# Sums of tail tokens on GpSimd, chunk-wide first products and a reshuffled tail in a weighted expert sum

## The chip, the cores and the metric

The kernel runs on one core of a Trainium2 chip. The metric is device time in microseconds (us) of one execution, the median of ten runs. A profile of one execution shows what each engine does: TensorE (PE; its weight loads are shown as PEld), VectorE (DVE), ScalarE (ACT), GpSimd (POOL) and SyncE (SP, which only issues transfers here). A name with a "q" behind it (DVEq, SPq, ACTq) is the engine's instruction queue. Transfers between the device memory (HBM) and the core's memory (SBUF) are moved by 16 DMA engines. TensorE writes its results to a memory of its own, PSUM.

## The reference

For each of 16 x 1024 = 16384 tokens there are the outputs of 8 experts, 512 numbers each, and 8 weights. The result is the weighted sum over the experts, in float32:

```python
batch, seq, n_experts, expert_dim = 16, 1024, 8, 512
weights = combine_weights[..., np.newaxis]
return np.sum(expert_outputs * weights, axis=2).astype(np.float32)
```

The input has 268.4 MB, the output 33.6 MB.

## The kernel before

Each of the 128 partitions handles 128 tokens. The first 120 of them (LOOP) are worked on in 12 rounds of R = 10, the last 8 (TAIL) in a tail. All instructions of all engines are written out by hand, with semaphores between the engines; each engine works through its list in order.

The tile ring holds the inputs of ten tokens per partition (10 x 8 x 512 numbers) and is the only input buffer. A round is loaded in three chunks of 4, 4 and 2 tokens (CHUNKS). SyncE issues a chunk's load (line 109) as soon as VectorE has finished the same chunk of the round before (semaphore done, raised once per finished token), so loads run ahead by as much as VectorE has already released. The tile acc holds 20 tokens' results, two halves for two rounds. ScalarE copies a round's weights to w_c (line 145) and issues the store of a finished half (line 99); before a half of acc is written again, its store must have landed (semaphore stored). In before VectorE itself waits for that, as for the chunks, in the helper take (line 173).

VectorE works on pairs of tokens. For the two tokens of a pair it alternates, expert by expert: the first product (line 204, one tensor operand and one weight per partition), then seven fused operations (line 187, called fused below: input times weight plus the sum so far). A fused operation waits for the semaphore step of the one two places earlier, which wrote the sum that it reads. Five pairs make a round: 80 instructions.

The tail's 8 tokens go to ring slots 0 to 7. SyncE issues their loads (line 119) one by one, each when the last round has released its slot. TensorE sums four of the eight terms of every tail token (line 163): the stationary operand is a diagonal matrix with one weight per token, made by ScalarE from an identity matrix (line 151; five buffers, made ahead as far as they are free), and the moving operand is the token's row; the sum is in ps, in PSUM. VectorE adds the other four by fused operations, the first of which reads ps. SyncE then issues the store of round 11 and four tail stores (line 123) of 4, 2, 1 and 1 tokens, in this order, on the same queue as the loads. GpSimd only builds the identity matrix at the start (lines 128 and 129).

Of the kernel before, what the change touches and what calls it, by code (L numbers as in the profile page):

```python
# [10 lines left out]
def kernel(  # L11
# [18 lines left out]
    nc = tc.nc  # L30
    fp32 = mybir.dt.float32
    mult, add = mybir.AluOpType.mult, mybir.AluOpType.add

    B, S, E, D = expert_outputs.shape
    T = B * S
    P = 128
    R = 10
# [4 lines left out]
    LOOP = GROUPS * G  # L42
    TAIL = T_P - LOOP
    ROUNDS = LOOP // R
# [11 lines left out]
    x_t = x[cut:T].rearrange("(p j) e d -> p j e d", j=TAIL)  # L56
# [1 line left out]
    o_t = o[cut:T].rearrange("(p j) d -> p j d", j=TAIL)  # L58


    pe_e = [4] * TAIL
    tail_loads = [(j, 1) for j in range(TAIL)]
    tail_stores = [(0, 4), (4, 2), (6, 1), (7, 1)]

    order = []
    for q in ((0, 1), (2,), (3,), (4,), (5,), (6,), (7,)):
        order += [(j, e) for e in range(pe_e[q[0]], E) for j in q]
    diags = [(j, e) for j in range(TAIL) for e in range(pe_e[j])]

    one = ctx.enter_context(tc.tile_pool(name="one", bufs=1))  # L70
# [1 line left out]
    ring = one.tile([P, R, E, D], fp32, name="ring")  # L72
    acc = one.tile([P, G, D], fp32, name="acc")
    w_t = one.tile([P, T_P, E], fp32, name="w_t")
    w_c = one.tile([P, G, E], fp32, name="w_c")
    ident = one.tile([P, P], fp32, name="ident")
    diag = one.tile([P, DIAGS, P], fp32, name="diag")
    ps = psum.tile([P, TAIL, D], fp32, name="ps")

    sem = tc.alloc_semaphore  # L80
    w_in = sem("w_in")
    w_set = [sem(f"w_set{h}") for h in range(2)]
    loaded = [sem(f"loaded{c}") for c in range(C)]
    stored = [sem(f"stored{h}") for h in range(2)]
    step = sem("step")
    done = sem("done")
    tail_in = [sem(f"tail_in{k}") for k in range(len(tail_loads))]
    tail_out = sem("tail_out")
    id_set = sem("id_set")
    diag_set = sem("diag_set")  # L90
    product = sem("product")

    def load_of(j):
        return [k for k, (q, m) in enumerate(tail_loads) if q <= j < q + m][0]

    def store(queue, n):
        h = n % 2
        queue.wait_ge(done, (n + 1) * R)
        queue.dma_start(
            out=o_g[n // 4, n // 2 % 2, :, h * R : h * R + R], in_=acc[:, h * R : h * R + R]  # L100
        ).then_inc(stored[h], 16)

    def loads_and_last_stores(sync):
        for n in range(ROUNDS):
            for c, (r, m) in enumerate(CHUNKS):
                if n:
                    sync.wait_ge(done, (n - 1) * R + r + m)
                g = n % 2 * R + r
                sync.dma_start(
                    out=ring[:, r : r + m], in_=x_g[n // 4, n // 2 % 2, :, g : g + m]  # L110
                ).then_inc(loaded[c], 16)
                if n == 0 and c == 0:
                    sync.dma_start(
                        out=w_t[:, 0:LOOP].rearrange("p (n m) e -> p n m e", m=M), in_=w_g
                    ).then_inc(w_in, 16)
                    sync.dma_start(out=w_t[:, LOOP:T_P], in_=w_x).then_inc(w_in, 16)
        for k, (j, m) in enumerate(tail_loads):
            sync.wait_ge(done, LOOP - R + j + m)
            sync.dma_start(out=ring[:, j : j + m], in_=x_t[:, j : j + m]).then_inc(tail_in[k], 16)
        store(sync, ROUNDS - 1)  # L120
        for j, m in tail_stores:
            sync.wait_ge(done, LOOP + j + m)
            sync.dma_start(out=o_t[:, j : j + m], in_=acc[:, j : j + m]).then_inc(tail_out, 16)
        sync.wait_ge(stored[(ROUNDS - 1) % 2], 16)
        sync.wait_ge(tail_out, 16 * len(tail_stores))

    def identity(gpsimd):
        gpsimd.memset(ident, 0.0).then_inc(id_set, 1)  # L128
        gpsimd.affine_select(  # L129
            out=ident,  # L130
            in_=ident,
            compare_op=mybir.AluOpType.not_equal,
            fill=1.0,
            base=0,
            pattern=[[-1, P]],
            channel_multiplier=1,
        ).wait_op(id_set, 1, "sem-ge").then_inc(id_set, 1)

    def weights_and_stores(scalar):
        scalar.wait_ge(w_in, 32)  # L140
        for n in range(ROUNDS):
            if n >= 2:
                store(scalar, n - 2)
            h = n % 2
            scalar.copy(  # L145
                out=w_c[:, h * R : h * R + R], in_=w_t[:, n * R : n * R + R]
            ).then_inc(w_set[h], 1)
        store(scalar, ROUNDS - 2)
        scalar.wait_ge(id_set, 2)
        for k, (j, e) in enumerate(diags):  # L150
            i = scalar.mul(out=diag[:, k % DIAGS], in_=ident, mul=w_t[:, LOOP + j, e : e + 1])  # L151
            i.then_inc(diag_set, 1)
            if k >= DIAGS:
                i.wait_op(product, k - DIAGS + 1, "sem-ge")

    def first_terms(tensor):
        came = set()
        for k, (j, e) in enumerate(diags):
            if load_of(j) not in came:
                came.add(load_of(j))  # L160
                tensor.wait_ge(tail_in[load_of(j)], 16)
            tensor.wait_ge(diag_set, k + 1)
            tensor.matmul(  # L163
                ps[:, j],
                lhsT=diag[:, k % DIAGS],
                rhs=ring[:, j, e],
                start=e == 0,
                stop=e == pe_e[j] - 1,
            ).then_inc(product, 1)

    def terms(vector):
        def take(s, v):
            vector.wait_ge(s, v).then_inc(s, -v)  # L173

        last = {}

        def count(i, g, e):

            if e == E - 1:
                i.then_inc(done, 1)  # L180
            else:
                i.then_inc(step, 1)
                last["all"] = last.get("all", 0) + 1
                last[g] = last["all"]

        def fused(g, e, weight, before):
            return vector.scalar_tensor_tensor(  # L187
                out=acc[:, g], in0=ring[:, g % R, e], scalar=weight, in1=before, op0=mult, op1=add
            )

        for h in range(2):
            vector.sem_inc(stored[h], 16)
        with nc.Fori(0, GROUPS, engines=OrderedEngineSet([vector.engine])):
            for h in range(2):
                take(w_set[h], 1)
                take(stored[h], 16)
                for c, (r, m) in enumerate(CHUNKS):
                    take(loaded[c], 16)
                    for q in range(h * R + r, h * R + r + m, 2):
                        for e in range(E):  # L200
                            for g in (q, q + 1):
                                weight = w_c[:, g, e : e + 1]
                                if e == 0:
                                    i = vector.tensor_scalar_mul(  # L204
                                        out=acc[:, g], in0=ring[:, g % R, 0], scalar1=weight
                                    )
                                else:
                                    i = fused(g, e, weight, acc[:, g])
                                    i.wait_op(step, last[g], "sem-ge")
                                count(i, g, e)  # L210
            take(step, last["all"])

        last.clear()
        came = set()
        take(stored[0], 16)
        vector.wait_ge(w_in, 32)
        for j, e in order:
            weight = w_t[:, LOOP + j, e : e + 1]
            if load_of(j) not in came:
                came.add(load_of(j))  # L220
                vector.wait_ge(tail_in[load_of(j)], 16)
            if e == pe_e[j]:
                i = fused(j, e, weight, ps[:, j])
                i.wait_op(product, sum(pe_e[: j + 1]), "sem-ge")
            else:
                i = fused(j, e, weight, acc[:, j])
                i.wait_op(step, last[j], "sem-ge")
            count(i, j, e)

    with tc.tile_critical(no_gpsimd_drain=True):  # L230
        loads_and_last_stores(nc.sync)
        identity(nc.gpsimd)
        weights_and_stores(nc.scalar)
        first_terms(nc.tensor)
        terms(nc.vector)
# [30 lines left out]
```

## Time and profile before

| what | value |
|---|---|
| median of 10 runs | 707.92 us (707.63 to 708.38) |
| the profiled execution's own time | 707.72 us |
| its span in the profile | 705.9 us |
| busy: VectorE | 628.2 us, 992 instructions |
| busy: TensorE | 31.4 us, 64 instructions |
| busy: ScalarE | 16.7 us, 45 instructions |
| busy: GpSimd | 0.7 us, 6 instructions |
| DMA | 302.5 MB, mean 429 GB/s |
| issues of the tail stores | from 684.7 to 700.4 us; 4.1 us (last) to 16.3 us (first) to landing |
| SyncE's final wait | ends at 704.4 us |

The span is the time between the first and the last event of the profiled execution; its own time has 1.8 us around it. In the page's groups a line reads: source line, engine, operation, output <- inputs, shapes, count | busy time in us, mean ns of one instruction | idle time of the engine just before, and what ended most of it. Consecutive VectorE instructions overlap in part, so that a group's time is less than count times mean; the spacing of the starts is the better price. The row of DMA shares divides the span in 40 slices, a digit is the busy share in tenths.

### The profile page before, as it was taken

To read this page: it belongs to the slowest core of one execution; us is meant where nothing else is said; L and a number is where in the kernel's file an instruction comes from. 1 tells how busy PE (TensorE), PEld (TensorE's weight loads), DVE (VectorE), ACT (ScalarE), POOL (GpSimd) and SP (SyncE) were. 2 spreads that over 40 slices of the span, in tenths; PEclk is the share of its full clock that TensorE was granted. 3 is DMA by queue.
4 is the path that set the end of the run, shared out by engine and by line. 5 is a ranking of instruction groups with operands and counts; after the bars stand their busy time and mean duration, and the time that the engine had idled before them with its cause. 6 is when DMAs were issued, how large, how long until landed. Compare 5 with 4: busy or idle time off the path is not lost. (4 is left out here: it accounts for less than half of the span.)

```text
span 705.9 us, 1388 instructions
## 1 busy us (share of the span) xinstructions
PE 31.4 (4%) x64; PEld 12.4 (2%) x64; DVE 628.2 (89%) x992; ACT 16.7 (2%) x45; POOL 0.7 (0%) x6
## 2 busy tenths in 40 slices
PE   0000000000000000000000000000000000000664
PEld 0000000000000000000000000000000000000221
DVE  0599989979979979979979989998997997997994
ACT  0000000000000000000000000000000000000230
POOL 0000000000000000000000000000000000000000
PEclk9999999999999999999999999999999999999998
DMA  9999999999999999999999999999999999999997
GB/s 416 386 472 420 406 424 447 416 444 436 432 433 449 438 405 438 436 424 473 434 395 452 417 427 438 468 395 467 420 445 416 431 430 461 427 432 404 430 428 331
DMA packets 9186, 302.53 MB, mean 429 GB/s; under 512 B 1120, under 2 KB 1504, under 8 KB 1888
## 3 DMA queue, kind: packets, MB, share of 16 engines
q1 hardware_dynamic: 7600, 273.68, 90.0%
q10 hardware_dynamic: 1584, 28.84, 9.5%
q14 instruction: 2, 0.02, 0.0%
HBM read 268.96 MB, written 33.55 MB: 429 GB/s over the span
## 5 line engine op out<-in xcount | busy, mean ns | idle before, releaser
L187 DVE SCALAR_TENSOR_TENSOR acc<-ring,w_c,acc 128x512 f32<-128x512 f32 x840 | 561.4, 744 | 0.0
L204 DVE TENSOR_SCALAR acc<-ring,w_c 128x512 f32<-128x512 f32 x120 | 52.6, 480 | 68.1 <-DVEq L173 68.1
L163 PE MATMUL ps<-ring,diag 128*128 128x512 f32 x64 | 31.4, 638 | 665.8 <-DMA ring<-in_expert_outputs_dram 665.8
L163 PEld LDWEIGHTS ps<-ring,diag 128*128 128x128 f32 x64 | 12.4, 202 | 684.0 <-DMA ring<-in_expert_outputs_dram 671.0
L187 DVE SCALAR_TENSOR_TENSOR acc<-ring,w_t,acc 128x512 f32<-128x512 f32 x24 | 17.6, 749 | 0.6
L145 ACT COPY w_c<-w_t 128x80 f32<-128x80 f32 x12 | 3.0, 258 | 559.9 <-DVE acc L187 537.8
L151 ACT ACTIVATE diag<-ident,w_t 128x128 f32<-128x128 f32 x32 | 12.4, 399 | 114.4 <-PE ps L163 60.2
L187 DVE SCALAR_TENSOR_TENSOR acc<-ring,w_t,ps 128x512 f32<-128x512 f32 x8 | 5.9, 742 | 3.4 <-PE ps L163 3.4
L145 ACT ACT_TABLE_LOAD x1 | 1.3, 1283 | 0.9 <-SPq L230 0.9
L129 POOL TENSOR_SCALAR_AFFINE_SELECT ident<-ident 128x128 f32<-128x128 f32 x1 | 0.3, 293 | 0.1
L128 POOL MEMSET ident<- 128x128 f32 x1 | 0.2, 206 | 0.5 <-SPq L230 0.5
L250 POOL MEMSET const-bfloat16-1.0<- 128x1 bf16 x1 | 0.1, 102 | 0.0
L250 POOL MEMSET const-uint8-127<- 128x1 uint8 x1 | 0.1, 102 | 0.0
L250 POOL MEMSET const-float32-0.0<- 128x1 f32 x1 | 0.1, 99 | 0.2 <-issue 0.2
L250 POOL MEMSET const-float32-1.0<- 128x1 f32 x1 | 0.1, 99 | 0.0
## 6 DMA issues: line engine op xcount, KB each, us to landing
ring<-in_expert_outputs_dram SPq DMA_DIRECT2D x12, 4096.0 KB, 34.4
out_dram<-acc ACTq DMA_DIRECT2D x11, 2560.0 KB, 26.5
ring<-in_expert_outputs_dram SPq DMA_DIRECT2D x8, 2048.0 KB, 30.1
out_dram<-acc SPq DMA_DIRECT2D x1, 2560.0 KB, 26.2
out_dram<-acc SPq DMA_DIRECT2D x1, 1024.0 KB, 16.3
out_dram<-acc SPq DMA_DIRECT2D x1, 512.0 KB, 11.1
out_dram<-acc SPq DMA_DIRECT2D x2, 256.0 KB, 5.5
w_t<-in_combine_weights_dram SPq DMA_DIRECT2D x1, 480.0 KB, 22.7
```

The costliest lines, as they stand in the source:

```text
L128: gpsimd.memset(ident, 0.0).then_inc(id_set, 1)
L129: gpsimd.affine_select(out=ident, in_=ident, compare_op=mybir.AluOpType.not_equal, fill=1.0, base=0, pattern=[[-1, P]], channel_multiplier ...
L145: scalar.copy(out=w_c[:, h * R : h * R + R], in_=w_t[:, n * R : n * R + R]).then_inc(w_set[h], 1)
L151: i = scalar.mul(out=diag[:, k % DIAGS], in_=ident, mul=w_t[:, LOOP + j, e : e + 1])
L163: tensor.matmul(ps[:, j], lhsT=diag[:, k % DIAGS], rhs=ring[:, j, e], start=e == 0, stop=e == pe_e[j] - 1,).then_inc(product, 1)
L187: return vector.scalar_tensor_tensor(out=acc[:, g], in0=ring[:, g % R, e], scalar=weight, in1=before, op0=mult, op1=add)
L204: i = vector.tensor_scalar_mul(out=acc[:, g], in0=ring[:, g % R, 0], scalar1=weight)
L250: nc = _bacc.Bacc("TRN2", target_bir_lowering=False, num_devices=1)
```

## The change

In the loop, the first products of a whole chunk become one multiply of two tensors, the second of them the weights repeated along the row (a broadcast). VectorE no longer waits for stores to land; ScalarE does, before it copies the weights into a half.

In the tail, GpSimd computes tokens 0 and 1 alone (new function pooled_tokens): eight products per token, written back into the ring, then a tree of 4, 2 and 1 adds; the semaphore pooled counts the finished tokens, and SyncE waits for both before the store of tokens 0 to 3. It begins when the even rounds' stores have all landed and the token is loaded. TensorE sums five terms of tokens 2 to 6 and four of token 7, VectorE the other three and four. For token 7 VectorE's own sum begins with a product and no longer waits for TensorE; TensorE's sum is added at the end.

```diff
--- before.py
+++ after.py
@@ -58,13 +58,9 @@
     o_t = o[cut:T].rearrange("(p j) d -> p j d", j=TAIL)
 
 
-    pe_e = [4] * TAIL
-    tail_loads = [(j, 1) for j in range(TAIL)]
+    POOLED = 2
+    pe_e = [0, 0, 5, 5, 5, 5, 5, 4]
     tail_stores = [(0, 4), (4, 2), (6, 1), (7, 1)]
-
-    order = []
-    for q in ((0, 1), (2,), (3,), (4,), (5,), (6,), (7,)):
-        order += [(j, e) for e in range(pe_e[q[0]], E) for j in q]
     diags = [(j, e) for j in range(TAIL) for e in range(pe_e[j])]
 
     one = ctx.enter_context(tc.tile_pool(name="one", bufs=1))
@@ -84,14 +80,13 @@
     stored = [sem(f"stored{h}") for h in range(2)]
     step = sem("step")
     done = sem("done")
-    tail_in = [sem(f"tail_in{k}") for k in range(len(tail_loads))]
+    tail_in = [sem(f"tail_in{j}") for j in range(TAIL)]
     tail_out = sem("tail_out")
     id_set = sem("id_set")
+    pool_step = sem("pool_step")
+    pooled = sem("pooled")
     diag_set = sem("diag_set")
     product = sem("product")
-
-    def load_of(j):
-        return [k for k, (q, m) in enumerate(tail_loads) if q <= j < q + m][0]
 
     def store(queue, n):
         h = n % 2
@@ -114,14 +109,16 @@
                         out=w_t[:, 0:LOOP].rearrange("p (n m) e -> p n m e", m=M), in_=w_g
                     ).then_inc(w_in, 16)
                     sync.dma_start(out=w_t[:, LOOP:T_P], in_=w_x).then_inc(w_in, 16)
-        for k, (j, m) in enumerate(tail_loads):
-            sync.wait_ge(done, LOOP - R + j + m)
-            sync.dma_start(out=ring[:, j : j + m], in_=x_t[:, j : j + m]).then_inc(tail_in[k], 16)
+        for j in range(TAIL):
+            sync.wait_ge(done, LOOP - R + j + 1)
+            sync.dma_start(out=ring[:, j], in_=x_t[:, j]).then_inc(tail_in[j], 16)
         store(sync, ROUNDS - 1)
         for j, m in tail_stores:
-            sync.wait_ge(done, LOOP + j + m)
+            if j < POOLED:
+                sync.wait_ge(pooled, POOLED)
+            sync.wait_ge(done, LOOP - POOLED + j + m)
             sync.dma_start(out=o_t[:, j : j + m], in_=acc[:, j : j + m]).then_inc(tail_out, 16)
-        sync.wait_ge(stored[(ROUNDS - 1) % 2], 16)
+        sync.wait_ge(stored[(ROUNDS - 1) % 2], 16 * ROUNDS // 2)
         sync.wait_ge(tail_out, 16 * len(tail_stores))
 
     def identity(gpsimd):
@@ -136,16 +133,42 @@
             channel_multiplier=1,
         ).wait_op(id_set, 1, "sem-ge").then_inc(id_set, 1)
 
+    def pooled_tokens(gpsimd):
+        gpsimd.wait_ge(w_in, 32)
+        gpsimd.wait_ge(stored[0], 16 * ROUNDS // 2)
+        steps = 0
+        for j in range(POOLED):
+            gpsimd.wait_ge(tail_in[j], 16)
+            for e in range(E):
+                gpsimd.tensor_scalar(
+                    out=ring[:, j, e],
+                    in0=ring[:, j, e],
+                    scalar1=w_t[:, LOOP + j, e : e + 1],
+                    scalar2=None,
+                    op0=mult,
+                ).then_inc(pool_step, 1)
+            for m in (4, 2, 1):
+                steps += {4: E, 2: 4, 1: 2}[m]
+                for k in range(m):
+                    y = acc[:, j] if m == 1 else ring[:, j, k]
+                    i = gpsimd.tensor_tensor(
+                        out=y, in0=ring[:, j, k], in1=ring[:, j, m + k], op=add
+                    )
+                    i.wait_op(pool_step, steps, "sem-ge")
+                    i.then_inc(pooled if m == 1 else pool_step, 1)
+
     def weights_and_stores(scalar):
         scalar.wait_ge(w_in, 32)
         for n in range(ROUNDS):
+            h = n % 2
             if n >= 2:
                 store(scalar, n - 2)
-            h = n % 2
+                scalar.wait_ge(stored[h], 16 * (n // 2))
             scalar.copy(
                 out=w_c[:, h * R : h * R + R], in_=w_t[:, n * R : n * R + R]
             ).then_inc(w_set[h], 1)
         store(scalar, ROUNDS - 2)
+        scalar.wait_ge(stored[0], 16 * ROUNDS // 2)
         scalar.wait_ge(id_set, 2)
         for k, (j, e) in enumerate(diags):
             i = scalar.mul(out=diag[:, k % DIAGS], in_=ident, mul=w_t[:, LOOP + j, e : e + 1])
@@ -154,11 +177,9 @@
                 i.wait_op(product, k - DIAGS + 1, "sem-ge")
 
     def first_terms(tensor):
-        came = set()
         for k, (j, e) in enumerate(diags):
-            if load_of(j) not in came:
-                came.add(load_of(j))
-                tensor.wait_ge(tail_in[load_of(j)], 16)
+            if e == 0:
+                tensor.wait_ge(tail_in[j], 16)
             tensor.wait_ge(diag_set, k + 1)
             tensor.matmul(
                 ps[:, j],
@@ -188,48 +209,60 @@
                 out=acc[:, g], in0=ring[:, g % R, e], scalar=weight, in1=before, op0=mult, op1=add
             )
 
-        for h in range(2):
-            vector.sem_inc(stored[h], 16)
         with nc.Fori(0, GROUPS, engines=OrderedEngineSet([vector.engine])):
             for h in range(2):
                 take(w_set[h], 1)
-                take(stored[h], 16)
                 for c, (r, m) in enumerate(CHUNKS):
                     take(loaded[c], 16)
-                    for q in range(h * R + r, h * R + r + m, 2):
-                        for e in range(E):
-                            for g in (q, q + 1):
-                                weight = w_c[:, g, e : e + 1]
-                                if e == 0:
-                                    i = vector.tensor_scalar_mul(
-                                        out=acc[:, g], in0=ring[:, g % R, 0], scalar1=weight
-                                    )
-                                else:
-                                    i = fused(g, e, weight, acc[:, g])
-                                    i.wait_op(step, last[g], "sem-ge")
-                                count(i, g, e)
+                    q = h * R + r
+                    i = vector.tensor_tensor(
+                        out=acc[:, q : q + m],
+                        in0=ring[:, r : r + m, 0],
+                        in1=w_c[:, q : q + m, 0:1].to_broadcast([P, m, D]),
+                        op=mult,
+                    )
+                    i.then_inc(step, 1)
+                    last["all"] = last.get("all", 0) + 1
+                    last.update((g, last["all"]) for g in range(q, q + m))
+                    for g in range(q, q + m, 2):
+                        for e in range(1, E):
+                            for k in (g, g + 1):
+                                i = fused(k, e, w_c[:, k, e : e + 1], acc[:, k])
+                                i.wait_op(step, last[k], "sem-ge")
+                                count(i, k, e)
             take(step, last["all"])
 
         last.clear()
-        came = set()
-        take(stored[0], 16)
-        vector.wait_ge(w_in, 32)
-        for j, e in order:
+        for j in range(POOLED, TAIL - 1):
+            for e in range(pe_e[j], E):
+                weight = w_t[:, LOOP + j, e : e + 1]
+                if e == pe_e[j]:
+                    i = fused(j, e, weight, ps[:, j])
+                    i.wait_op(product, sum(pe_e[: j + 1]), "sem-ge")
+                else:
+                    i = fused(j, e, weight, acc[:, j])
+                    i.wait_op(step, last[j], "sem-ge")
+                count(i, j, e)
+
+        j = TAIL - 1
+        for e in range(pe_e[j], E):
             weight = w_t[:, LOOP + j, e : e + 1]
-            if load_of(j) not in came:
-                came.add(load_of(j))
-                vector.wait_ge(tail_in[load_of(j)], 16)
             if e == pe_e[j]:
-                i = fused(j, e, weight, ps[:, j])
-                i.wait_op(product, sum(pe_e[: j + 1]), "sem-ge")
+                i = vector.tensor_scalar_mul(out=acc[:, j], in0=ring[:, j, e], scalar1=weight)
+                i.wait_op(tail_in[j], 16, "sem-ge")
             else:
                 i = fused(j, e, weight, acc[:, j])
                 i.wait_op(step, last[j], "sem-ge")
-            count(i, j, e)
+            count(i, j, -1)
+        vector.wait_ge(step, last[j])
+        i = vector.tensor_tensor(out=acc[:, j], in0=acc[:, j], in1=ps[:, j], op=add)
+        i.wait_op(product, len(diags), "sem-ge")
+        count(i, j, E - 1)
 
     with tc.tile_critical(no_gpsimd_drain=True):
         loads_and_last_stores(nc.sync)
         identity(nc.gpsimd)
+        pooled_tokens(nc.gpsimd)
         weights_and_stores(nc.scalar)
         first_terms(nc.tensor)
         terms(nc.vector)
```

## The prediction

> **What bounds the kernel now.** I read the page first: the row of DMA shares and the groups of instructions.
>
> ```profile
> span 705.9 us, 1388 instructions
> ...
> DVE  0599989979979979979979989998997997997994
> ...
> DMA  9999999999999999999999999999999999999997
> ...
> HBM read 268.96 MB, written 33.55 MB: 429 GB/s over the span
> ...
> L187 DVE SCALAR_TENSOR_TENSOR acc<-ring,w_c,acc 128x512 f32<-128x512 f32 x840 | 561.4, 744 | 0.0
> L204 DVE TENSOR_SCALAR acc<-ring,w_c 128x512 f32<-128x512 f32 x120 | 52.6, 480 | 68.1 <-DVEq L173 68.1
> ...
> L187 DVE SCALAR_TENSOR_TENSOR acc<-ring,w_t,ps 128x512 f32<-128x512 f32 x8 | 5.9, 742 | 3.4 <-PE ps L163 3.4
> ...
> L129 POOL TENSOR_SCALAR_AFFINE_SELECT ident<-ident 128x128 f32<-128x128 f32 x1 | 0.3, 293 | 0.1
> L128 POOL MEMSET ident<- 128x128 f32 x1 | 0.2, 206 | 0.5 <-SPq L230 0.5
> L250 POOL MEMSET const-bfloat16-1.0<- 128x1 bf16 x1 | 0.1, 102 | 0.0
> ...
> out_dram<-acc ACTq DMA_DIRECT2D x11, 2560.0 KB, 26.5
> ```
>
> VectorE is busy 89% and the DMA engines all the time. The busy times of one whole round of ten tokens decide between them (columns: stretch, its length, then busy time and count of each engine, clock, DMA share, GB/s):
>
> ```profile
> 316.42:370.83 54.41, 0.00 (x0) 0.00 (x0) 50.42 (x80) 0.26 (x1) 0.00 (x0) 1.00 1.00 434
> ```
>
> The DMA share is 1.00 while VectorE works 50.4 of 54.4 us. The missing 4.0 us are its wait for a chunk (68.1 us in all, 25.0 of them before the first chunk). The loop is bound by transfer; VectorE has 4 us to spare per round. The tail comes from the timeline (start, duration) and the chain that ended last:
>
> ```profile
> 643.03 0.88 DVE L204 TENSOR_SCALAR acc<-ring,w_c 128x512 f32<-128x512 f32 x2 [4.01 <-DVEq L173]
> 643.83 9.36 DVE L187 SCALAR_TENSOR_TENSOR acc<-ring,w_c,acc 128x512 f32<-128x512 f32 x14
> 653.10 0.87 DVE L204 TENSOR_SCALAR acc<-ring,w_c 128x512 f32<-128x512 f32 x2
> ...
> 658.29 9.15 PE L163 MATMUL ps<-ring,diag 128*128 128x512 f32 x16 [658.29 <-DMA ring<-in_expert_outputs_dram]
> ...
> 673.34 0.35 SPq L99 DMA_DIRECT2D out_dram<-acc  x1
> ```
> ```profile
> 663.27 30.18 DMA ring<-in_expert_outputs_dram
> ...
> 693.50 3.71 PE ps L163 x8
> ...
> 697.24 0.76 DVE acc L187
> ...
> 699.60 0.75 DVE acc L187
> ```
>
> Tail token 0 has landed at 658.29, the last one at 693.46. Then come four matrix products (3.71), four chained VectorE operations (to 700.35) and a store that lands 4.1 us after its issue. Note that from 643 to 673 VectorE works without a pause, and that it is still computing the last round when the first tail token arrives.
>
> From the starts: a pair of tokens takes 10.07 us, 0.79 for its two one-operand products (0.40 each), 9.27 for 14 fused operations (0.663 each). In the tail the chained fused ones start 0.776 apart.
>
> **The change, part by part.**
>
> Loop products. Three broadcast multiplies replace ten products per round. The new form is not in the trace; it is between the one-operand row (0.40 per token, no change) and the fused row with two tensor operands (0.663 per token, 10 x 0.26 = 2.6 us more per round). I take the fused row, as it too reads two tensors. The 4.0 us chunk wait hides it: a chunk is freed later by at most 2.6 us, but at that moment other chunks' loads are still queued. Without that cover 12 rounds would cost 31 us. Below nothing I find no path: bytes and their order stay.
>
> Waits moved from VectorE to ScalarE. The copy of a round's weights now waits until the store of two rounds earlier has landed, 26.5 us after issue. Behind it on ScalarE stands the next store's issue, due a round (54.4 us) later, and VectorE needs the copy at that time too: 28 us to spare, cost 0. After the loop, ScalarE's first five diagonals wait for the round 10 store (issued 618.91, landed about 645.4); the first is now used by token 2, landed about 668. Cost 0.
>
> Matrix products. 29 instead of 32; a token of five takes 3.71 + 0.86 = 4.57 us against 4.9 between landings. The last token: token 6, landed 688.63, is summed at 693.2, its three fused operations end at 695.5. Then VectorE does token 7's product and three fused ones (0.45 + 2.33, to 698.3) beside the matrix products (to 697.2), and one add (0.75): 699.1 instead of 700.35. VectorE gains 1.25 us. The second-last 256 KB store landed at 702.4 and the last at 704.4, so the queue gives back perhaps a third: 0.9 us, bounds 0 and 1.4.
>
> GpSimd's two tokens. 16 products and 14 adds, 128x512, begin at 658.29. From the POOL rows: filling 128 elements instead of 1 costs 104 ns more, 0.83 ns an element, so 0.53 us for 512 without any reading; the select, which reads and compares, 1.52 ns, so 0.88 us. A product lies between: I take 0.70. A second operand costs VectorE a factor of 0.663/0.40; I use 1.5 for the add: 1.05 us, bounds 0.88 (no surcharge on the select) and 1.65 (its reading paid twice). Sum 16 x 0.70 + 14 x 1.05 = 25.9 us, bounds 20.8 and 37.2. Undisturbed it ends at 684.2, at most 695.5. Behind it on SP's queue are all four tail stores; the first is needed when the load of token 7 (693.46) and the 2.6 MB store of round 11 (landed 699.5) are through, so about 697.5 is early enough. By itself GpSimd's work is hidden. (The Trainium skill, GPSIMD Engine Reference, section Performance versus the Vector engine, gives about 1.8 cycles per element at 1.2 GHz for a good one-input loop and 2.6 for two inputs; the estimate from it is 27.9 us in place of 25.9. No run here shows it.)
>
> What these instructions do to VectorE is the dear question. No row shows the two at work together: GpSimd's last instruction starts at 1.22 us, VectorE's first at 24.99. The lower bound is nothing: the fused operation takes 744 ns in the loop and 742 to 749 in the tail, with TensorE and ScalarE running beside it. The upper bound is that they take turns. I take turns: the 0.40 and 0.663 us rows say that VectorE pays for its second operand's reading, so reading limits it already, and GpSimd would read the same tile at that time. It is a judgement, and I give it six chances in ten.
>
> (The Trainium skill says so outright: SBUF — State Buffer, section Who interferes with whom, has a VectorE instruction with two SBUF inputs and a GpSimd instruction that reads SBUF exclude each other for the length of the instruction. It speaks against this change; by the rule the sum is the one below, without it 707.0. The trace of before cannot show either.)
>
> Sum with turns, from 658.29. VectorE's loop remainder is 673.24 - 658.29 = 14.95, plus 1.05 and 0.53 for the dearer chunk products (four tokens, then two): 16.5. Tail operations with both operands in SBUF: 13 x 0.776 + 0.45 = 10.5; the five that read PSUM I count as running beside GpSimd. GpSimd 25.9. Together 52.9, so 711.2, and the last add ends at 712.0: 11.6 us after 700.35. On the way: tail loads 6 and 7 are issued at about 670 instead of 663 (664.2 and eight products of GpSimd), which costs nothing, as load 5 landed only at 683.7; the round 11 store goes out at about 693 instead of 673.34, just as the loads run dry; the first tail store follows GpSimd at about 702. All before 712, so the last store is what ends it, 4.1 us after issue as now. The profiled execution took 707.72 (span 705.9 and 1.8 around it), the median is 0.20 higher: 707.72 + 11.6 + 0.20 = 719.5. GpSimd's bounds give 714.4 and 730.8.
>
> **The rivals.**
> Independent engines: GpSimd doesn't hold VectorE up. For it: TensorE and ScalarE don't. Against it: the second operand's price. 707.92 - 0.9 = 707.0, between 706.5 and 707.9; not slower. It decides from the point where GpSimd costs VectorE less than the time that the tail leaves it idle: after 673 it has 20 operations, 15.5 us, in 26 us.
> Half of it: they share by the element and both stretch, VectorE by a third. The remainder of 16.5 us becomes 22, to 680.3, and the 20 operations 20.7, so 701.0: with waits between them 708 to 712.
> A lost cover: the broadcast multiply above the fused row. From 4.0 us more per round (0.40 per token above the product) each further us costs 12 us in all; at 0.85 per token 6 us over the loop, on top of the rest. Nothing in the rows is so slow.
>
> **How the numbers follow.** Turns 0.60, independent 0.27, half 0.10, lost cover or another 0.03. A change of 0.2% is 1.4 us, about what a measurement of this kernel can tell. Turns, nine tenths of half, and the lost cover are slower: 0.71 less a little for turns that are cheap, 0.69. Faster needs the upper bound of the last token's gain: 0.04. Same: 0.27. The likeliest time is 719.5, its own range 712 to 728; the range for all goes from 706.8, which takes in most of the independent case, to 727.
>
> **What would show it.** Turns: fused operations between 658 and 700 start about 1.4 us apart instead of 0.66; the last round ends near 693; GpSimd's last add near 702; last VectorE operation near 712. Independent: last round ends near 674, last operation at 699. The loop: rounds stay at 54.4 us with a shorter chunk wait of 1.4 us or more. The prediction is wrong if VectorE's spacing stays at 0.66 beside GpSimd, if GpSimd's products are far from 0.70 us, or if the loop's rounds lengthen.

## The result and the profile after

The changed kernel takes 722.67 us (median of 8 runs, 722.31 to 723.63) against 707.99 us (median of 28). The ratio is 1.0209, 95% interval 1.0200 to 1.0218: 14.7 us slower. The profiled execution took 721.94 us with a span of 719.9, 14.0 more than the span before.

The page of the changed kernel, its first lines and the groups that are new or changed (after the bar: busy us, mean ns of one, idle before):

```profile
span 719.9 us, 1286 instructions
...
DVE  0699999989989989989989989989989989989970
...
POOL 0000000000000000000000000000000000004995
...
DMA  9999999999999999999999999999999999999972
...
POOL 7%; DMA 4%; DVE 2%; issue 0%; POOLq 0%
...
L208 DVE SCALAR_TENSOR_TENSOR acc<-ring,w_c,acc 128x512 f32<-128x512 f32 x840 | 562.6, 748 | 1.3
L218 DVE TENSOR_TENSOR acc<-ring,w_c 128x2048 f32<-128x2048 f32 (+1 forms) x36 | 69.5, 1931 | 45.4 <-DVEq L194 45.4
L143 POOL TENSOR_SCALAR ring<-ring,w_t 128x512 f32<-128x512 f32 x16 | 33.4, 2106 | 657.0 <-DMA ring<-in_expert_outputs_dram 657.0
...
L154 POOL TENSOR_TENSOR ring<-ring 128x512 f32<-128x512 f32 x12 | 16.6, 1415 | 0.3
...
L208 DVE SCALAR_TENSOR_TENSOR acc<-ring,w_t,acc 128x512 f32<-128x512 f32 x13 | 14.3, 1103 | 0.5
```

The loss is all at the end: the last two slices of the DMA row, 9 and 7 before, now read 7 and 2. The chain that ended last now runs through POOL (7%), which was not in it before. The loop's time is unchanged. One whole round, by busy times,

```profile
316.00:370.40 54.40, 0.00 (x0) 0.00 (x0) 52.24 (x74) 0.26 (x1) 0.00 (x0) 1.00 1.00 434
```

still takes 54.4 us at a DMA share of 1.00. VectorE works 52.24 instead of 50.42 us in it, the chunk wait has shrunk to about 2.05, and the DMA engines do not notice.

The timeline of the tail (start, duration, engine, count) shows who is last, and the list of SyncE's own waits says the same:

```profile
658.49 19.66 POOL L143 TENSOR_SCALAR ring<-ring,w_t 128x512 f32<-128x512 f32 x8 [656.99 <-DMA ring<-in_expert_outputs_dram]
663.18 1.22 DVE L218 TENSOR_TENSOR acc<-ring,w_c 128x1024 f32<-128x1024 f32 x1
664.44 12.28 DVE L208 SCALAR_TENSOR_TENSOR acc<-ring,w_c,acc 128x512 f32<-128x512 f32 x14
...
698.56 0.69 DVE L258 TENSOR_TENSOR acc<-acc,ps 128x512 f32<-128x512 f32 x1
...
710.60 1.26 POOL L154 TENSOR_TENSOR acc<-ring 128x512 f32<-128x512 f32 x1
711.89 3.07 SPq L120 DMA_DIRECT2D out_dram<-acc  x4
```
```profile
SPq L120 <- POOL acc L154: 28.4, 1, 28.4
```

VectorE finishes at 699.25, 1.1 us earlier than before. GpSimd finishes at 711.86. SyncE stands 28.4 us before the first tail store waiting for it, with the other three stores behind, and the last of them lands 6.5 us after GpSimd's last add. Between 700 and 710 us nothing is transferred at all (columns as for the round above: DMA share 0.00, while POOL is busy for 9.84 us):

```profile
700.00:710.00 10.00, 0.00 (x0) 0.00 (x0) 0.00 (x0) 0.00 (x0) 9.84 (x8) 0.55 0.00 0
```

So the kernel is slower because GpSimd is late, not because VectorE is.

Two single rows, one instruction each, show what happened to GpSimd:

```profile
658.49 7.35 POOL L143 TENSOR_SCALAR ring<-ring,w_t 128x512 f32<-128x512 f32 x1 [656.99 <-DMA ring<-in_expert_outputs_dram]
```
```profile
665.82 1.77 POOL L143 TENSOR_SCALAR ring<-ring,w_t 128x512 f32<-128x512 f32 x1
```

The first product takes 7.35 us, while VectorE's fused operations go on at their usual 0.66 us spacing as if nothing were there; it ends at 665.84, 1.4 us after VectorE's chunk product (663.18 to 664.40). From then on each product goes with two fused operations, one of which is stretched to 1.17 us: 1.76 us for the three.

Two questions follow. How much of GpSimd's 53.4 us is its own speed, and how much is VectorE's doing? And did the rest of the change give anything?

### The profile page after: what moved, and what is told of

Read it like the earlier page. It is cut to its first block, busy times and chain, and to the rows that moved or that the text cites. A ratio compares the mean times of both kernels' runs of the same rounds, so it can differ in the third digit from the quotient of the medians.

```text
span 719.9 us, 1286 instructions
## 1 busy us (share of the span) xinstructions
PE 28.1 (4%) x58; PEld 11.9 (2%) x58; DVE 649.5 (90%) x896; ACT 15.5 (2%) x42; POOL 53.6 (7%) x36
## 5 line engine op out<-in xcount | busy, mean ns | idle before, releaser
L218 DVE TENSOR_TENSOR acc<-ring,w_c 128x2048 f32<-128x2048 f32 (+1 forms) x36 | 69.5, 1931 | 45.4 <-DVEq L194 45.4
L143 POOL TENSOR_SCALAR ring<-ring,w_t 128x512 f32<-128x512 f32 x16 | 33.4, 2106 | 657.0 <-DMA ring<-in_expert_outputs_dram 657.0
L184 PE MATMUL ps<-ring,diag 128*128 128x512 f32 x58 | 28.1, 648 | 668.1 <-DMA ring<-in_expert_outputs_dram 668.1
L154 POOL TENSOR_TENSOR ring<-ring 128x512 f32<-128x512 f32 x12 | 16.6, 1415 | 0.3
L208 DVE SCALAR_TENSOR_TENSOR acc<-ring,w_t,acc 128x512 f32<-128x512 f32 x13 | 14.3, 1103 | 0.5
L208 DVE SCALAR_TENSOR_TENSOR acc<-ring,w_t,ps 128x512 f32<-128x512 f32 x5 | 3.7, 742 | 2.5 <-PE ps L184 2.5
L154 POOL TENSOR_TENSOR acc<-ring 128x512 f32<-128x512 f32 x2 | 2.9, 1432 | 0.2
## 6 DMA issues: line engine op xcount, KB each, us to landing
out_dram<-acc ACTq DMA_DIRECT2D x11, 2560.0 KB, 26.7
```

The source lines that it names most:

```text
L143: gpsimd.tensor_scalar(out=ring[:, j, e], in0=ring[:, j, e], scalar1=w_t[:, LOOP + j, e : e + 1], scalar2=None, op0=mult,).then_inc(pool_s ...
L154: i = gpsimd.tensor_tensor(out=y, in0=ring[:, j, k], in1=ring[:, j, m + k], op=add)
L184: tensor.matmul(ps[:, j], lhsT=diag[:, k % DIAGS], rhs=ring[:, j, e], start=e == 0, stop=e == pe_e[j] - 1,).then_inc(product, 1)
L208: return vector.scalar_tensor_tensor(out=acc[:, g], in0=ring[:, g % R, e], scalar=weight, in1=before, op0=mult, op1=add)
L218: i = vector.tensor_tensor(out=acc[:, q : q + m], in0=ring[:, r : r + m, 0], in1=w_c[:, q : q + m, 0:1].to_broadcast([P, m, D]), op=mult,)
```

## The experiments

**GpSimd's tokens taken back.** Two kernels: one without GpSimd's work, one with one token for it.

```diff
-    POOLED = 2
-    pe_e = [0, 0, 5, 5, 5, 5, 5, 4]
+    POOLED = 0
+    pe_e = [5, 5, 5, 5, 5, 5, 5, 4]
```


> GpSimd sums no tail token; TensorE sums five terms of tokens 0 to 6 and four of token 7, VectorE the rest. All else as in the changed kernel. Theory A (all of the loss comes from GpSimd's two tokens): the time falls below the kernel before by what the side-by-side last token gives, 707.0 us, between 706.5 and 707.9; VectorE's last operation near 699.1. Theory B (the broadcast products or the moved waits cost something as well): above 708.5.


Measured: 707.86 us against 707.95, ratio 0.9995 (0.9986 to 1.0004). The time lies within theory A's range, and theory B falls. Of the 0.9 us hoped for from the last token the medians show 0.09; the interval reaches from 1.0 us faster to 0.3 slower, so this run alone does not exclude them.

```diff
-    POOLED = 2
-    pe_e = [0, 0, 5, 5, 5, 5, 5, 4]
+    POOLED = 1
+    pe_e = [0, 5, 5, 5, 5, 5, 5, 4]
```


> GpSimd sums token 0 alone, TensorE and VectorE token 1 too. In the changed kernel's trace token 0 was finished at 689.2 us, and 697.5 was worked out as early enough for the first tail store. Theory A (the end is GpSimd's late last add, seven stores behind it): 707.0 to 708 us, GpSimd again done near 689. Theory C (VectorE's lengthened operations matter too): each of the 15 GpSimd instructions costs VectorE some 0.4 to 0.9 us, so its last operation comes after 700.5 and the time is above 708.5.


Measured: 707.64 us, ratio 0.9993 (0.9984 to 1.0002). Theory A holds, theory C falls. GpSimd finished its token at 690.4, and that delay costs nothing. The whole 14.7 us hang on the second token, which pushes GpSimd's end past what the queued stores cover.

**The loop's changes alone.** The kernel before with the broadcast product and the moved waits.

```diff
-                    for q in range(h * R + r, h * R + r + m, 2):
-                        for e in range(E):
+                    i = vector.tensor_tensor(
+                        out=acc[:, q : q + m],
+                        in0=ring[:, r : r + m, 0],
+                        in1=w_c[:, q : q + m, 0:1].to_broadcast([P, m, D]),
+                        op=mult,
+                    )
...
```


> The kernel before with the loop's two changes alone (broadcast product per chunk; ScalarE waits for the stores). The changed kernel's trace shows 52.2 us of VectorE work in a round of 54.4 against 50.4 before. Theory A: covered by the transfers, 707.9 us within 0.3. Theory B: the loop's changes cost something: above 708.5. The difference of this run to the run without GpSimd is what the tail's other changes give: 0.9 us expected.


Measured: 708.47 us, ratio 1.0008 (0.9999 to 1.0017): no difference that can be told. It lies just above theory A's 707.9 within 0.3 and just below theory B's 708.5. The difference to the kernel without GpSimd's tokens, expected at 0.9 us, is 0.61, within what the two intervals leave open; traces settle it below ("Where the last token's gain went").

**GpSimd undisturbed.** Its two tokens begin when VectorE is through.

```diff
         gpsimd.wait_ge(stored[0], 16 * ROUNDS // 2)
+        gpsimd.wait_ge(done, LOOP - POOLED + TAIL)
```


> GpSimd's two tokens begin only when VectorE has finished everything (about 699.3 us). Gives the undisturbed length of GpSimd's work. Theory A (VectorE holds GpSimd up): products 1.54 us apart and adds 1.22, as in the undisturbed rows of the changed kernel, 42.3 us in all, against 53.4 there; last add ends near 741.6, span about 749.6. Theory F (GpSimd's products are as slow as seen, 1.7 to 2.4 us, by themselves): about 53 us, span above 755.


Measured (one execution): span 749.0. GpSimd's timeline:

```profile
698.51 12.34 POOL L144 TENSOR_SCALAR ring<-ring,w_t 128x512 f32<-128x512 f32 x8 [697.01 <-DVE acc L259]
710.93 7.47 POOL L155 TENSOR_TENSOR ring<-ring 128x512 f32<-128x512 f32 x6
718.49 1.26 POOL L155 TENSOR_TENSOR acc<-ring 128x512 f32<-128x512 f32 x1
719.72 12.33 POOL L144 TENSOR_SCALAR ring<-ring,w_t 128x512 f32<-128x512 f32 x8
732.14 7.47 POOL L155 TENSOR_TENSOR ring<-ring 128x512 f32<-128x512 f32 x6
739.69 1.26 POOL L155 TENSOR_TENSOR acc<-ring 128x512 f32<-128x512 f32 x1
```

A product every 1.54 us, an add every 1.22, both tokens in 42.4 us (698.51 to 740.95): theory A holds, theory F falls. In the changed kernel they took 53.4. So GpSimd alone would have ended at 658.49 + 42.4 = 700.9; what runs beside it adds the other 10.9 us, and the runs below show that this is VectorE. The first product here shows nothing special, so the 7.35 us are no price of a first call.

**What VectorE reads.** VectorE's partial sums of the tail tokens stay in PSUM, so that its tail operations read one operand from SBUF instead of two.

```diff
                 if e == pe_e[j]:
-                    i = fused(j, e, weight, ps[:, j])
+                    i = fused(j, e, weight, ps[:, j], ps[:, j])
...
-                    i = fused(j, e, weight, acc[:, j])
+                    i = fused(j, e, weight, ps[:, j], None if e == E - 1 else ps[:, j])
```
(The added last argument is where the sum goes; without it, to acc. Token 7's own sum is kept in a free slot of ps in the same way.)


> As the changed kernel, but VectorE keeps its partial sums of the tail tokens in PSUM, so that no tail operation of it has two operands in SBUF. Theory D (GpSimd and VectorE exclude each other only when VectorE reads two operands from SBUF): nothing changes until the last round ends near 676.5; after that GpSimd's instructions start 1.54 us (products) and 1.22 us (adds) apart as they do when VectorE is idle, VectorE's fused ones 0.78 apart; GpSimd ends at about 677.9 + 8.6 + 12.4 + 8.9 = 708 instead of 711.9, the time is about 719. Theory E (they disturb each other whatever VectorE reads, or it is the DMA traffic or TensorE that slows GpSimd): GpSimd's spacing stays as it was and it ends near 711.9; time 722 to 723.


Measured: 718.89 us, ratio 1.0157 (1.0141 to 1.0172). GpSimd's timeline:

```profile
658.42 20.05 POOL L143 TENSOR_SCALAR ring<-ring,w_t 128x512 f32<-128x512 f32 x8 [656.92 <-DMA ring<-in_expert_outputs_dram]
678.56 7.53 POOL L154 TENSOR_TENSOR ring<-ring 128x512 f32<-128x512 f32 x6
686.17 1.27 POOL L154 TENSOR_TENSOR acc<-ring 128x512 f32<-128x512 f32 x1
687.41 12.36 POOL L143 TENSOR_SCALAR ring<-ring,w_t 128x512 f32<-128x512 f32 x8
699.86 7.48 POOL L154 TENSOR_TENSOR ring<-ring 128x512 f32<-128x512 f32 x6
707.41 1.26 POOL L154 TENSOR_TENSOR acc<-ring 128x512 f32<-128x512 f32 x1
```

Up to 678 nearly all is as in the changed kernel (one product takes 0.58 us longer). After that, GpSimd runs at its undisturbed spacing (7.53 against 7.47 us for six adds, 12.36 against 12.34 for eight products) right beside VectorE, TensorE and the transfers, and VectorE's operations keep their 0.75 us. Theory D holds, theory E falls: for the fused operations it is the second operand from SBUF that collides with GpSimd's work. The edit moves VectorE's results to PSUM as well, but that is not what counts: in the changed kernel the five fused operations that read ps and write acc keep 0.73 to 0.75 us beside GpSimd.

One row of the changed kernel does not fit a rule that two operands from SBUF are always needed. Token 7's first product on VectorE reads one tensor from SBUF; beside GpSimd's products it takes 0.92 us, and in the kernel without GpSimd's tokens 0.48:

```profile
694.86 0.92 DVE L251 TENSOR_SCALAR acc<-ring,w_t 128x512 f32<-128x512 f32 x1
```
```profile
694.64 0.48 DVE L251 TENSOR_SCALAR acc<-ring,w_t 128x512 f32<-128x512 f32 x1
```

Why this form is held up too, no run here shows.

**Why the first product takes 7 us.** GpSimd begins after VectorE's last chunk but one.

```diff
         gpsimd.wait_ge(stored[0], 16 * ROUNDS // 2)
+        gpsimd.wait_ge(done, LOOP - 2)
```


> As the changed kernel, but GpSimd begins only when VectorE has finished the tokens before the last chunk (about 663.2 us instead of 658.5). Theory K (its first product did nothing from 658.5 until VectorE paused around the chunk product, because VectorE's fused operations overlap each other without a gap): the first product again ends near 665.8, all that follows stays, the last add again near 711.9, span near 719.9. Theory L (the first product was at work or loading something all the time): it ends 7.3 us after its later start, near 670.6, and the span grows by about 4.7 us.


Measured (one execution): span 720.3.

```profile
664.39 2.29 POOL L144 TENSOR_SCALAR ring<-ring,w_t 128x512 f32<-128x512 f32 x1 [662.89 <-DVE acc L209]
```

It starts 5.9 us later and is through 0.8 us later; the last add ends at 712.2 instead of 711.9. This execution's loads landed about 0.84 us later as a whole; counted from the landing of the last tail load, the first product ends at the same point in both (26.7 us before it). Theory K holds, theory L falls. The head start was worth nothing: the first product had stood still. Next, one gap per pair of tokens in VectorE's stream:

```diff
-                                i.wait_op(step, last[k], "sem-ge")
+                                i.wait_op(step, last["all" if (e, k) == (6, g) else k], "sem-ge")
```


> As the changed kernel, but in each pair of tokens one fused operation (expert 6, first token) waits for the operation just before it instead of the one two places earlier: one small gap of about 0.1 us per pair. The loop has 2 us per round to spare for it. Theory K (GpSimd gets in at the first gap of VectorE): the first product gets in near 660.6 and ends near 662.2 instead of 665.8; everything after it comes some 3.5 us earlier, last add near 708.4, time about 719.2. Theory M (only the chunk product lets it in, or the pause was not what counted): no change, 722.7.


Measured: 720.04 us, ratio 1.0171 (1.0154 to 1.0188).

```profile
658.61 3.70 POOL L143 TENSOR_SCALAR ring<-ring,w_t 128x512 f32<-128x512 f32 x1 [657.11 <-DMA ring<-in_expert_outputs_dram]
```

The first product ends at 662.3, 3.5 us earlier, 1.4 us behind the added gap at about 660.9; theory K holds, M falls. The last add comes only 1.75 us earlier (710.1), as the third product now meets the chunk product and takes 1.06 us longer (2.83 us), and the first token's adds and the second's products together take 0.7 us more.

**The price in the steady loop.** No GpSimd tokens; instead 30 products and then 30 adds on a tile of its own, beside the loop from the end of the fourth round.

```diff
+        gpsimd.memset(diag[:, 0:4], 1.0).then_inc(pool_step, 1)
+        gpsimd.wait_ge(done, 4 * R)
+        for k in range(60):
+            if k < 30:
+                i = gpsimd.tensor_scalar(
+                    out=diag[:, 0:4],
...
```


> The kernel without GpSimd's tokens, but GpSimd works on a small tile of its own beside the steady loop from the end of the fourth round: 30 products in place with a weight per partition, then 30 adds, each waiting for the one before. Theory A (VectorE's back-to-back fused operations keep GpSimd out until VectorE pauses): the first product does not end before VectorE's next pause or chunk product, 7 us or more; after it one GpSimd instruction goes with two fused ones, some 1.75 us per product, and a pair of fused ones starts about 0.43 us later than undisturbed; the rounds beside GpSimd take 2 to 4 us more of VectorE's time each. Theory J (fair turns): every GpSimd instruction waits for one fused operation at most, VectorE for every GpSimd instruction, and VectorE's rounds rise far above 54.4 us.


Measured (one execution): 733.83 us. VectorE's timeline:

```profile
268.24 24.50 DVE L225 SCALAR_TENSOR_TENSOR acc<-ring,w_c,acc 128x512 f32<-128x512 f32 x28
...
293.91 17.85 DVE L225 SCALAR_TENSOR_TENSOR acc<-ring,w_c,acc 128x512 f32<-128x512 f32 x14
```

28 fused operations beside products take 24.5 us (18.64 undisturbed), 14 mostly beside adds 17.85 (9.36). Where the rhythm is steady, a product goes with two fused operations in 1.76 us, an add with one in 1.445. VectorE loses 1.76 - 2 x 0.663 = 0.43 us per product and 1.445 - 0.663 = 0.78 per add; GpSimd loses 0.22 and 0.22. These adds read one place twice; the tokens' adds, which read two places, go with one fused operation of the loop in 1.67 us (next run), and there VectorE loses 1.0 and GpSimd 0.45. GpSimd's tile here is one that VectorE does not touch, so the hold-up does not need a shared tile. Neither theory was right as put: there is a rhythm as in A, but the first product did not wait 7 us (it came in behind the chunk product that was just running, 3.45 us in all), and the 2 to 4 us of VectorE's time per round that A expected were 18: the two rounds took 140.5 us (239.10 to 379.55) where VectorE alone needs 2 x 52.2, and the kernel 26 us more.

**The form of the product.** A multiply of two tensors in place of one weight per partition.

```diff
-                gpsimd.tensor_scalar(
...
-                    scalar1=w_t[:, LOOP + j, e : e + 1],
-                    scalar2=None,
-                    op0=mult,
+                    in1=w_t[:, LOOP + j, e : e + 1].to_broadcast([P, D]),
+                    op=mult,
```


> GpSimd's products as a multiply of two tensors, the second the weight repeated along the row, in place of the product with one weight per partition. Theory G (it is the form with a weight per partition that costs 1.54 us): 1.22 us like the adds, 16 x 0.32 = 5.1 us less in all, end near 706.8, time about 717.5. Theory H (a multiply or the writing back in place is what is slow): 1.54 us as before, time 722.7.


Measured: 720.48 us, ratio 1.0180 (1.0163 to 1.0197). A product now goes with one fused operation in 1.445 us, so GpSimd is done at 710.3 instead of 711.9, and VectorE pays: the last 14 fused operations of the loop take 21.58 us instead of 12.28, and its last add comes at 708.6. GpSimd's adds beside the loop's fused operations come 1.67 us apart. How long such a product takes alone this run can't tell (a later one does); neither theory's time came.

**The order of the stores.**

```diff
-    tail_stores = [(0, 4), (4, 2), (6, 1), (7, 1)]
+    tail_stores = [(2, 2), (4, 2), (6, 1), (7, 1), (0, 2)]
...
+            else:
+                sync.wait_ge(done, LOOP - POOLED + j + m)
```


> The store of GpSimd's two tokens goes last in SyncE's queue; tokens 2 to 7 are stored without it. GpSimd's end stays at 711.9. Theory A (four stores queue behind GpSimd's last add): they cost 711.9 to 718.4 now; one 512 KB store alone lands about 4.1 us after its issue, so 716.3 and 720.4 in time, 2.3 less. Theory I (the last add alone matters, the stores go out together): within 0.5 of 722.7.


Measured: 718.45 us, ratio 1.0148 (1.0131 to 1.0165), 4.2 us less than the changed kernel. The lone store landed 2.6 us after its issue, where 4.1 were expected. Theory A holds, with more than its price.

**Where the last token's gain went.** Without GpSimd, VectorE's last operation ends at 698.28, 2.07 us before that of the kernel before, and the time is the same. Of the 2.07 us, 0.82 come from the tail's loads, which landed that much earlier in this execution (the last at 692.64 against 693.46). Counted from that landing, VectorE ends after 5.64 us instead of 6.89, and the last store lands after 10.98 instead of 10.97. In the kernel with the loop's changes alone it lands after 10.97, with one token on GpSimd after 10.97. VectorE's 1.25 us do not reach the end at all. The kernel without GpSimd's tokens, and without the stores of tail tokens 0 to 6:

```diff
-    tail_stores = [(0, 4), (4, 2), (6, 1), (7, 1)]
+    tail_stores = [(7, 1)]
```


> The kernel without GpSimd's tokens, with the stores of tail tokens 0 to 6 left out (those rows of the output are not written); only token 7 is stored after round 11. Theory N (VectorE's earlier end gave nothing measurable because the queued stores of the tail, 2.1 MB, still had to drain): the last store, issued near 698.3, lands within 3 us, as the lone store did after GpSimd; span about 702.5, time about 704.3. Theory O (the last store's own way is what ends it, whatever stands before it): 707.9.


Measured: 703.73 us, ratio 0.9942 (0.9925 to 0.9958), 4.1 us below the same kernel with all stores; the stores left out are 1.84 MB, 4.2 us at 434 GB/s. The last store landed 2.0 us after its issue, against 5.3 in the kernel with all stores, and 7.65 us after the last tail load against 10.98. Of the 3.9 us between the two profiled executions, 3.3 lie there. Theory N holds: with all stores the end is bound by the queue draining, and VectorE's earlier end is spent waiting in it.

**All causes mended, both tokens on GpSimd.** Sums in PSUM, two-tensor products, GpSimd's store last (the three edits above).


> Three of the earlier edits together, GpSimd keeping both tokens: VectorE's partial sums in PSUM, GpSimd's products as a multiply of two tensors, the store of GpSimd's tokens last in SyncE's queue. If the causes are GpSimd's own speed, the hold-up by VectorE and the queued stores, they add: first product ends near 665.8, seven more at 1.45 us beside the last fused operations of the loop (676), seven adds at 1.22 (684.7), then, undisturbed, eight products at 1.22 (694.4) and seven adds (703.2); a 512 KB store landing 2.6 us later ends it: span about 707.5, time about 709.3. If a product of two tensors takes longer than an add when undisturbed (1.5 us), the last add comes at 705.5 and the time is 711.6. If GpSimd's multiplies hold VectorE up so much that VectorE ends last, after 705: above 711.


Measured: 711.04 us, ratio 1.0046 (1.0029 to 1.0063). Second token on GpSimd's timeline:

```profile
687.86 8.02 POOL L144 TENSOR_TENSOR ring<-ring,w_t 128x512 f32<-128x512 f32 x8
695.96 7.50 POOL L154 TENSOR_TENSOR ring<-ring 128x512 f32<-128x512 f32 x6
703.53 1.26 POOL L154 TENSOR_TENSOR acc<-ring 128x512 f32<-128x512 f32 x1
```

Beside VectorE operations with one operand in SBUF, which left GpSimd undisturbed above, a two-tensor product takes 1.00 us, less than an add (1.22) and less than the form with a weight per partition (1.54). The last add ends at 704.79 where 703.2 was expected: the first token's adds fall beside VectorE's stretched loop end, so that token is done at 687.9 instead of 684.7. None of the three cases put down beforehand fits in full; the time lies 1.7 us above the first one's sum. The three edits together win back 11.6 of the 14.7 us, somewhat more than their single gains added up (3.8, 2.2 and 4.2, together 10.2). What remains fits two tokens being too much for GpSimd in this tail, as one costs nothing. No version tried that stores every row is measurably faster than the kernel before.

## Why the prediction was right, and where it was not

The time (719.5 predicted, range 706.8 to 727, 722.67 measured), the side, and the cause in the large, GpSimd and VectorE in each other's way, were right. The path to the number was not, and that the number came so close is luck. By one of the prediction's own signs of being wrong, GpSimd's products far from 0.70 us, it was wrong.

- Loop products: right in kind. 2.29 us for four tokens lies between the bounds (1.60 and 2.65), 1.8 us more per round where 2.6 were taken, covered by the chunk wait.
- Waits moved to ScalarE, and matrix products: right, no cost seen.
- Last token: right, VectorE gains the 1.25 us that were worked out, counted from the last landing. What of them reaches the end was put at 0.9 us with bounds 0 and 1.4 (the upper one more than VectorE's own gain); the traces give 0, the lower bound: the last store lands 10.97 to 10.98 us after the last tail load either way.
- GpSimd's own time: the term was mis-sized. 25.9 us were summed, bounds 20.8 and 37.2; it is 42.4. The add (1.22) lies within its bounds; the product with one weight per partition (1.54, taken as 0.70) lies far above its upper bound of 0.88. The bound came from a select over 128 elements, another instruction: it bounded nothing.
- "By itself GpSimd's work is hidden" fails with it. Alone it would have ended at 700.9, later than the 697.5 that was early enough, so even the rival of independent engines would have been slower: with the stores' 6.5 us the span would be about 708.9, an estimate from these numbers.
- "I take turns" is the step that failed in its form. VectorE was charged with all of GpSimd's time and put last, at 712.0. It lost only about 7.4 us (the lengths of its fused operations beyond 0.75 from 664 on, added up), most of it absorbed in waits for landings and matrix products, and ended at 699.25. GpSimd ended last, at 711.86. Two errors, GpSimd too fast and the two engines too strictly in turn, cancelled: with GpSimd's true 42.4 us in place of 25.9 the prediction's own sum would have given 736.0 us, outside its range.
- The rivals: "half of it", given one chance in ten, has the form that the runs show beside products. Both engines stretch, VectorE by 0.43 us on two fused operations of 1.33, the third that it named. Its time of 708 to 712 was too low, as it let VectorE end last. "A lost cover" falls: the rounds stayed at 54.4 us.
- The stores: the prediction let the last store land 4.1 us after the last operation. With four stores behind GpSimd's it was 6.5, the larger part of the 3.2 us between 719.5 and 722.67.

The rule that was quoted against the change, from the Trainium skill (SBUF — State Buffer, section Who interferes with whom), stands in its first half: fused operations with two SBUF inputs collide with GpSimd, and those with one do not (six adds in 7.53 against 7.47 us). Its other half, exclusion for the length of the instruction, does not fit: a product and two fused operations would take 1.54 + 2 x 0.663 = 2.87 us one after another, and take 1.76. The same skill's figure of 1.8 cycles per element for a one-input loop (GPSIMD Engine Reference, section Performance versus the Vector engine), 0.77 us as an estimate, is half of the 1.54 measured for the form with a weight per partition; its 2.6 cycles for two inputs, 1.11 us, come near the add's 1.22.

## What to carry to other kernels

Before work goes to an idle engine, price its instructions in the very form that will run, and ask what else is reading the same memory then: here GpSimd's 42 us became 53 beside a VectorE that streams two SBUF operands, and cost VectorE 0.4 to 1.0 us per instruction in return, where VectorE was streaming. Ask too what queues behind the handed-over work: putting its store last in the queue was worth 4.2 us with no other change. And where a queue of stores drains at the end, an engine that finishes earlier may gain nothing until the bytes shrink, as here.

## What the runs showed that was not expected

- A stream of overlapping fused operations shuts GpSimd's reading out entirely: 7.35 us for one product, shortened to 3.70 when one fused operation starts 0.78 us after the one before it instead of 0.66. Once let in, GpSimd keeps a steady rhythm with it (a product and two fused operations in 1.76 us).
- GpSimd's hold on VectorE is shorter than its instruction: 0.43 us per product with one tensor operand (of 1.54), 0.78 per add that reads one place twice and 1.0 per add of two places (of 1.22). That each operand's reading is what holds VectorE fits these numbers roughly but was not tested apart.
- On GpSimd a product with the weight repeated as a second tensor takes 1.00 us, with one weight per partition 1.54.
